# A two-direction gated recurrence: one direction of two heads per tile instead of both directions of one head

## The chip, the cores and the metric

The program runs on one core of one Trainium2 chip. The metric is device time in microseconds (us) for one execution of the whole program. TensorE is called PE, its weight loads PEld, VectorE DVE, ScalarE ACT, GpSimd POOL; SP issues most DMAs.

## The reference, cut to what matters

The program is a trunk of two layers over 512 latent and 256 context tokens of width 1024. Each layer applies a norm, one input projection, four token mixers (A to D), an output projection and a mixture of experts. The change lies in mixer A, a gated linear recurrence with 4 heads of 64 channels, run forwards and backwards over the tokens:

```python
def step(S, inp):                      # one chunk of 64 tokens, one direction
    qc, kc, fc, vc = inp
    b = jnp.cumsum(fc, axis=2)         # log decays
    o_inter = einsum('bhtk,bhkv->bhtv', qc * exp(b), S)
    decay = exp(where(causal, b[t] - b[s], -inf))
    attn = einsum('bhtk,bhsk,bhtsk->bhts', qc, kc, decay)
    o_intra = einsum('bhts,bhsv->bhtv', attn, vc)
    S_new = exp(b_last) * S + einsum('bhsk,bhsv->bhkv', kc * exp(b_last - b), vc)
...
o_f, _ = hgrn_chunk_scan(qh, k_f, lf_f, ih, s_cf)
o_b, _ = hgrn_chunk_scan(rev(qh), rev(k_b), rev(lf_b), rev(ih), s_cb)
out = hgrn_readout(o_f + rev(o_b), g, norm_g)
```

The query is the same in both directions; forget gates and keys differ. Layer 0 computes outputs for all 768 tokens (NQ = 768), layer 1 for the 512 latent ones (NQ = 512); states run over 768 in both.

## The kernel before, in words

Channels lie on partitions, tokens along the free axis. `Proj.cols` (line 1281) makes 128 columns of the input projection at a time; an `ev` function moves them out of PSUM. For the recurrence these are two tiles of values, two of queries, four of gates and two of output gates. The queries of each head are written twice (lines 1530 and 1531): rows 0 to 63 of a tile `QQ[h]` for the forward direction, rows 64 to 127 for the backward one. Gate tile h holds the forward channels of head h in rows 0 to 63 and its backward channels in rows 64 to 127; from it come the decays `F[h]` and the keys `K[h]`.

`hgrn` then works in five steps.

1. Level 0, per head: `scores` multiplies keys and queries of each 128 tokens (line 234, NP = 6 or 4 matmuls of 128 rows, into a double PSUM bank from a ring of two), DVE keeps the diagonal (line 239), and the queries are multiplied by F (line 246).
2. Six levels with half-blocks of 1, 2, 4, ... 32 tokens; at each, four heads. ACT builds `kx`: the keys of the half-block that a direction reads from, and zeros in the other half (lines 256 and 257, two instructions each on 64 partitions). `scores` multiplies; DVE copies the valid pairs into the score tile A with a predicated copy (line 241). Then queries and keys are decayed in place: the forward rows on DVE, the backward rows on POOL, a query multiply (line 265) and a key multiply (line 266) each. DVE merges the block decays T (line 268).
3. Per pair of heads and head: the keys are transposed (line 278), copied by ACT (line 279), multiplied by the values with 64 rows at a time (line 284), and DVE scans the states over 12 chunks, forwards in rows 0 to 63 and backwards in rows 64 to 127 (line 291, 22 instructions per head).
4. Values times scores (line 300) and states times queries (line 303) give the outputs in PSUM.
5. Square, head sum (line 309), reciprocal root and gate (lines 194 to 200, 312, 313).

One fp32 matmul of the program appears in the trace as two records, each with its weight load. A scheduler puts the instructions of each engine in a fixed order: work that is later in the program fills an engine where the earlier work is expected to wait. In the levels this filling is the modulation (line 1175, `more(STEPH)`) and the Hyena projection (line 1281). Both follow `hgrn` in the program.

Of the kernel before, what the change touches and what calls it, by code (L numbers as in the profile page):

```python
# [25 lines left out]
class Region:  # L26
    """First-fit allocation of columns of one SBUF tile, in program order."""
# [26 lines left out]
class Arena:  # L54
    """The regions that are open at a point of the program; later ones are filled first."""
# [27 lines left out]
class Scope:  # L83
    """Named rings of arena buffers that live together."""
# [30 lines left out]
class Env:  # L115
    """Memory and small helpers shared by the stages."""
# [34 lines left out]
    def px(self):  # L151
        """One bank, of the two kinds in turn."""
# [6 lines left out]
    def pf(self):  # L159
        """One bank, of the single and double kinds in turn."""  # L160
# [6 lines left out]
    def load(self, tag, ap, bufs=1):  # L167
        """Arena copy of a DRAM array [128 or fewer, ...]."""
# [11 lines left out]
def split(n):  # L180
    """Column ranges of at most one PSUM bank."""
# [7 lines left out]
def rsqrt_wide(E, src, n, scale, tag, tags=None, width=NTOK):  # L189
    """1/sqrt(scale*src + EPS) for src [128, n] (PSUM): Ln/Exp estimate and one Newton step."""  # L190
# [13 lines left out]
# ---------------------------------------------------------------- HGRN  # L204
# [4 lines left out]
def hgrn_masks():  # L209
    """Valid (s, t) pairs of a 128-token chunk pair: the diagonal, then each level, both directions."""  # L210
# [7 lines left out]

def hgrn(E, need_ctx, QQ, F, K, V, SG, gn, oT):
# [7 lines left out]
    A, QR, T = {}, {}, {}  # L227
    fw, bw = slice(0, 64), slice(64, 128)

    def scores(h, lev, kx, q):  # L230
        ps = E.p2()
        for p in range(NP):
            c = slice(p * 128, p * 128 + 128)
            nc.tensor.matmul(ps[:, c], kx[:, c], q[:, c], start=True, stop=True)  # L234
        m = masks[:, lev, :].unsqueeze(1).to_broadcast([P, NP, 128])
        pv = ps[:, :NQ].rearrange("p (a t) -> p a t", t=128)
        if lev == 0:
            A[h] = E.t("hA", NTOK, bufs=4)
# [1695 lines left out]
```

## Time and profile before

| | us |
|---|---|
| median of three runs | 2461.23 |
| lowest and highest | 2455.57, 2463.83 |
| profiled execution, first to last instruction (its span) | 2456.8 |
| recurrence levels, layer 0 (258 to 322) | 64 |
| recurrence levels, layer 1 (1498.5 to 1553.5) | 55 |

The page of the profile gives no time of that execution beside its span; the span lies inside the runs shown, 4.4 us under their median. In the profile "busy" is the time in which an engine worked on at least one instruction, so instructions that overlap count once; a mean duration counts each instruction in full. Matmul ends are modelled.

### The profile page before, as it was taken

What the parts mean: (1) busy time and instruction counts of PE and PEld (TensorE: products, weight loads), DVE (VectorE), ACT (ScalarE), POOL (GpSimd) and SP (SyncE); (2) the same over time, 40 slices, a digit from 0 to 9 for tenths busy, and PEclk for the clock granted to TensorE, in tenths of its full rate; (3) what the DMA queues carried; (4) which work ended last, traced back from release to release, by engine and by line L of the source; (5) the groups of instructions that cost most, each with busy time, mean ns of one, the idle gap of its engine ahead of it and who ended that gap; (6) DMA issues with size and microseconds to landing.
All of it is one profiled execution on the core that took longest, in us unless ns stands there. A gap on an engine that the chain in (4) does not pass through costs nothing.

```text
span 2456.8 us, 32343 instructions
## 1 busy us (share of the span) xinstructions
PE 2056.0 (84%) x11460; PEld 1197.4 (49%) x11460; DVE 1053.5 (43%) x2495; ACT 606.9 (25%) x1200; POOL 587.5 (24%) x477
## 2 busy tenths in 40 slices
PE   5889888998999588887777498899999588877776
PEld 1557667865679333322222286676668433222221
DVE  6760985546865622221111437754684611111111
ACT  3434632243541100000000235324352110000000
POOL 1552722312003211211111236331101212111111
PEclk9999999999999699999999799999999699999998
DMA  6434424301231899999999524431233799999996
GB/s 244 156 121 163 172 81 148 112 26 52 84 130 70 290 385 376 405 402 404 400 402 400 216 86 155 134 125 35 73 116 116 283 391 409 411 407 410 410 406 263
DMA packets 139315, 581.56 MB, mean 237 GB/s; under 512 B 23984, under 2 KB 47873, under 8 KB 88630
## 3 DMA queue, kind: packets, MB, share of 16 engines
q1 hardware_dynamic: 124054, 555.89, 58.4%
q0 software_dynamic: 15008, 22.36, 3.8%
q8 instruction: 151, 2.47, 0.4%
q14 instruction: 102, 0.84, 0.1%
HBM read 554.17 MB, written 36.80 MB: 241 GB/s over the span
## 4 chain that ended last, share of the span: by engine, by line
DMA 20%; PE 19%; another core or an unknown queue 18%; DVE 8%; issue 2%; ACT 1%; POOL 1%; SPq 0%; ACTq 0%; POOLq 0%; DVEq 0%
DMA acc<-arena 8%; DMA out_dram<-arena 7%; PE pw L1281 6%; DMA arena<-h2d,arena 4%; PE pb L993 3%; PE pw L1773 2%; PE pb L1020 1%; PE pb L607 1%; PE pb L509 1%; PE pb L527 1%; DVE arena L265 1%; DMA arena<-in_w_out 1%; DVE arena L266 1%; PE pb L1748 0%
## 5 line engine op out<-in xcount | busy, mean ns | idle before, releaser
L993 PE MATMUL pb<-side,arena 128*64 128x512 f32 x1224 | 287.1, 603 | 43.0 <-DMA side<-in_w_moe 40.9
L997 DVE COPY arena<-pb 128x512 f32<-128x512 f32 x67 | 46.4, 692 | 496.0 <-PE pb L993 496.0
L993 PE MATMUL pb<-arena 128*64 128x512 f32 x920 | 217.1, 605 | 40.5 <-DMA arena<-in_w_moe 36.9
L1009 ACT ACTIVATE arena<-pb 128x256 f32<-128x256 f32 x67 | 25.7, 383 | 900.1 <-PE pb L1006 900.1
L1257 POOL TENSOR_TENSOR wl<-side,wh 128x1024 fp32r<-128x1024 f32 x52 | 126.4, 2430 | 380.2 <-ACT wh L1256 225.9
L993 PEld LDWEIGHTS pb<-side,arena 128*64 128x64 f32 x1224 | 81.2, 137 | 243.4 <-issue 126.6
L1281 PE MATMUL pw<-hh,wh 128*128 128x512 f32 (+1 forms) x720 | 170.7, 371 | 2.6 <-ACT arena L1180 1.2
L1281 PE MATMUL pw<-hh,wl 128*128 128x512 f32 (+1 forms) x720 | 163.1, 359 | 0.0
L1024 DVE SCALAR_TENSOR_TENSOR arena<-pb,arena 128x512 f32<-128x512 f32 x67 | 50.3, 751 | 262.9 <-PE pb L1020 253.0
L1281 PE MATMUL pw<-hl,wh 128*128 128x512 f32 (+1 forms) x720 | 160.5, 357 | 0.0
L993 PEld LDWEIGHTS pb<-arena 128*64 128x64 f32 x920 | 62.1, 138 | 189.0 <-issue 100.2
L1020 PE MATMUL pb<-side,arena 128*64 128x512 f32 x576 | 134.3, 606 | 23.6 <-DVE arena L1010 21.5
L1033 POOL DMA_INDIRECT acc<-arena x35 | 55.2, 1577 | 384.6 <-DVE arena L1028 344.5
L1281 PEld LDWEIGHTS pw<-hh,wh 128*128 128x128 f32 x720 | 120.4, 194 | 36.1 <-issue 12.5
L1020 PE MATMUL pb<-arena 128*64 128x512 f32 x496 | 117.2, 613 | 21.7 <-DVE arena L1010 20.6
L1281 PEld LDWEIGHTS pw<-hl,wh 128*128 128x128 f32 x720 | 118.2, 190 | 25.0 <-issue 8.9
L1281 PEld LDWEIGHTS pw<-hh,wl 128*128 128x128 f32 x720 | 117.6, 189 | 24.6 <-issue 9.7
L1033 POOL DMA_INDIRECT out_dram<-arena x32 | 50.9, 1590 | 311.1 <-DVE arena L1024 299.1
L971 POOL DMA_INDIRECT arena<-h2d,arena x67 | 69.8, 1042 | 187.0 <-issue 65.6
L1777 POOL TENSOR_TENSOR arena<-arena 128x256 f32<-128x256 f32 x40 | 30.4, 759 | 294.3 <-DVE arena L1776 185.5
L234 PE MATMUL pa<-arena 128*128 128x128 f32 x560 | 75.6, 283 | 18.5 <-ACT arena L257 6.0
L1006 PE MATMUL pb<-ident,arena 128*128 128x128 f32 x268 | 42.2, 280 | 56.3 <-DVE arena L997 55.4
(368 smaller groups left out, 3594.3 us busy)
## 6 DMA issues: line engine op xcount, KB each, us to landing
side<-in_w_moe SPq DMA_DIRECT2D x215, 1024.0 KB
arena<-in_w_moe SPq DMA_DIRECT2D x169, 1024.0 KB
arena<-in_w_ada SPq DMA_DIRECT2D x53, 512.0 KB
side<-in_w_in SPq DMA_DIRECT2D x52, 512.0 KB
side<-in_w_ada SPq DMA_DIRECT2D x43, 512.0 KB
arena<-in_w_out SPq DMA_DIRECT2D x16, 512.0 KB
arena<-in_x SPq DMA_DIRECT2D x12, 512.0 KB
spd<-arena SPq DMA_DIRECT2D x23, 256.0 KB
```

The lines of the kernel that those rows point to most:

```text
L234: nc.tensor.matmul(ps[:, c], kx[:, c], q[:, c], start=True, stop=True)
L971: E.gathered = nc.gpsimd.indirect_dma_start(out=xg, out_offset=None, in_=h2d, in_offset=bass.IndirectOffsetOnAxis(ap=gi, axis=0), **(dict( ...
L993: nc.tensor.matmul(pg[64 * s:64 * s + 64], xT[:, j // 4, j % 4, :], W[j // 2][:, (j % 2) * 1024 + s * 512:(j % 2) * 1024 + s * 512 + 512], ...
L997: nc.vector.tensor_copy(gu, pg)
L1006: nc.tensor.transpose(pt[:, c * 128:(c + 1) * 128], gu[:, c * 128:(c + 1) * 128], E.c["ident"])
L1020: nc.tensor.matmul(pd[64 * s:64 * s + 64], hT[:, c, :], W[4 + c // 2][:, (c % 2) * 1024 + s * 512:(c % 2) * 1024 + s * 512 + 512], start=( ...
L1024: nc.vector.scalar_tensor_tensor(y, pd, w[0], g2[0], op0=ALU.mult, op1=ALU.mult)
L1033: E.nc.gpsimd.indirect_dma_start(out=acc, out_offset=bass.IndirectOffsetOnAxis(ap=si, axis=0), in_=y, in_offset=None, compute_op=ALU.add, ...
L1257: (nc.vector if k % 2 else nc.gpsimd).tensor_sub(lo, src, hi.bitcast(F32))
L1281: nc.tensor.matmul(ps[:, :n], w[:, j, :], h[:, j, a:a + n], start=(i == 0), stop=(i == 23))
L1773: nc.tensor.matmul(ps[:, :256], o_[:, k, tt], w[:, k, :], start=(i == 0), stop=(i == 23))
L1777: nc.gpsimd.tensor_add(x1[t][:, cc], x1[t][:, cc], tmp)
```

## The change

A tile now holds one direction of two heads: `K[2*pair]` is the forward keys of both heads of a pair (head 0 in rows 0 to 63, head 1 in rows 64 to 127), `K[2*pair+1]` their backward keys; F likewise. The columns of the weights and the lower-bound logits are put in that order on the host. The queries come out of the projection as they are, one ACT copy per chunk, two tiles instead of four; a second copy per pair arises when they are multiplied by F.

At level 0 each head's scores are the sum of two products of 64 rows, forward and backward keys. At each level a merged key tile `mk` and a merged query tile `mq` are built by four ACT copies on 128 partitions per pair: the forward keys of the first half-blocks beside the backward keys of the second, and the reverse for queries. Nothing is zeroed. The scores are matmuls of 64 rows per head that alternate between the two heads, into both double banks of the ring. Query decays all run on DVE, key decays all on POOL, with 128 partitions each. After the levels, the transposed keys, the last block decays and the queries are rearranged back to both directions of one head by ACT copies (`kts`, `Th`, `QB`), since the scan is as before.

```diff
-    def scores(h, lev, kx, q):
-        ps = E.p2()
+    def scores(pair, lev, terms):
+        ps = [E.p2() for _ in range(2)]
         for p in range(NP):
             c = slice(p * 128, p * 128 + 128)
-            nc.tensor.matmul(ps[:, c], kx[:, c], q[:, c], start=True, stop=True)
+            for s, rows in enumerate(half):
+                for i, (k, q) in enumerate(terms):
+                    nc.tensor.matmul(ps[s][:, c], k[rows, c], q[rows, c], start=(i == 0), stop=(i == len(terms) - 1))
...
-    for h in range(4):
-        scores(h, 0, K[h], QQ[h])
-        QR[h] = QQ[h]
-        nc.vector.tensor_mul(QR[h][:, :NQ], QQ[h][:, :NQ], F[h][:, :NQ])
-        T[h] = F[h]
+    QR = {}
+    for pair in range(2):
+        f, b = 2 * pair, 2 * pair + 1
+        scores(pair, 0, [(K[f], Q[pair]), (K[b], Q[pair])])
+        QR[f], QR[b] = E.t("hQR", NTOK, bufs=2), Q[pair]
+        nc.vector.tensor_mul(QR[f][:, :NQ], Q[pair][:, :NQ], F[f][:, :NQ])
+        nc.vector.tensor_mul(QR[b][:, :NQ], Q[pair][:, :NQ], F[b][:, :NQ])
+        T[f], T[b] = F[f], F[b]
...
-        for h in range(4):
-            kx = E.t("hKX", NTOK, bufs=2)
...
-            for rows, src in ((fw, 0), (bw, 1)):
-                nc.scalar.copy(xv[rows, :nq, src, :], kv[rows, :nq, src, :])
-                nc.scalar.activation(xv[rows, :nq, 1 - src, :], kv[rows, :nq, src, :], AF.Copy, scale=0.0)
-            scores(h, li + 1, kx, QR[h])
...
-            for rows, mine, other in ((fw, 1, 0), (bw, 0, 1)):
-                eng = nc.vector if rows is fw else nc.gpsimd
...
-                eng.tensor_mul(qv[rows, :nq, mine, :], qv[rows, :nq, mine, :], tq)
-                eng.tensor_mul(kv[rows, :, other, :], kv[rows, :, other, :], tk)
-            T[h] = F[h][:, :nb] if hb < 32 else E.t("hT", nb, bufs=4)
-            nc.vector.tensor_mul(T[h], tv[:, :, 0], tv[:, :, 1])
+        for pair in range(2):
+            f, b = 2 * pair, 2 * pair + 1
+            mq, mk = E.t("hKT", NTOK, bufs=2), E.t("hKX", NTOK, bufs=2)
+            for dst, first, second in ((mk, K[f], K[b]), (mq, QR[b], QR[f])):
+                for i, src in enumerate((first, second)):
+                    nc.scalar.copy(blocks(dst)[:, :nq, i, :], blocks(src)[:, :nq, i, :])
+            scores(pair, li + 1, [(mk, mq)])
+            for z, mine in ((f, 1), (b, 0)):
...
+                nc.vector.tensor_mul(qv[:, :nq, mine, :], qv[:, :nq, mine, :], tq)
+                nc.gpsimd.tensor_mul(kv[:, :, 1 - mine, :], kv[:, :, 1 - mine, :], tk)
+                T[z] = F[z][:, :nb] if hb < 32 else E.t("hT", nb, bufs=4)
+                nc.vector.tensor_mul(T[z], tv[:, :, 0], tv[:, :, 1])
...
     for pair in range(2):
...
+        for r, rows in enumerate(half):
+            z = 2 * pair + r
+            ps = E.p2()
+            for t in range(6):
+                nc.tensor.transpose(ps[:, t * 128:(t + 1) * 128], K[z][:, t * 128:(t + 1) * 128], ident)
+            pv = ps[:, :NTOK].rearrange("p (t s c) -> p t s c", t=6, s=2)
+            for s in range(2):
+                nc.scalar.copy(kts[s][:, :, r], pv[:, :, s])
+                nc.scalar.copy(Th[s][rows], T[z][half[s]])
...
+            QB[s] = K[h]
+            for r, rows in enumerate(half):
+                nc.scalar.copy(QB[s][rows, :NQ], QR[2 * pair + r][half[s], :NQ])
...
-                def ev(ps, a, n):
-                    for s_ in range(2):
-                        q = QQ[2 * pair + s_]
-                        nc.vector.tensor_copy(q[0:64, a:a + n], ps[64 * s_:64 * s_ + 64])
-                        nc.scalar.copy(q[64:128, a:a + n], ps[64 * s_:64 * s_ + 64])
-                pr.cols(COL["q"] + pair, both, ev)
+                pr.cols(COL["q"] + pair, both, lambda ps, a, n: nc.scalar.copy(QQ[pair][:, a:a + n], ps))
```

## Rows read from the trace of the kernel before

**Rows 1.** Busy time by stretch: PE, PEld, DVE, ACT, POOL, clock, DMA share, GB/s.

```profile
258.00:322.00 64.00, 53.79 (x451) 39.23 (x451) 64.00 (x91) 45.87 (x98) 49.53 (x54) 1.00 0.47 163
322.00:346.00 24.00, 18.81 (x191) 15.16 (x190) 18.49 (x57) 4.59 (x7) 3.17 (x2) 0.86 0.23 79
...
1498.50:1553.50 55.00, 45.39 (x374) 28.66 (x366) 55.00 (x99) 37.40 (x100) 44.62 (x54) 1.00 0.60 199
1553.50:1580.00 26.50, 25.95 (x205) 18.59 (x204) 18.03 (x52) 6.74 (x10) 4.55 (x2) 1.00 0.39 124
```

**Rows 2.** Groups by line and shape, 258 to 322 (busy us, mean ns, idle before).

```profile
L234 PE MATMUL pa<-arena 128*128 128x128 f32 x277 | 36.7, 282 | 9.9 <-ACT arena L257 3.2 <-DVE arena L241 2.3 <-DVE arena L268 1.8
...
L266 POOL TENSOR_TENSOR arena<-arena 64x384 f32<-64x384 f32 x22 | 23.3, 1057 | 11.9 <-ACT arena L257 9.1 <-DVE arena L266 2.2 <-DVE arena L265 0.6
L241 DVE COPY_PREDICATED arena<-hmask,pa 128x768 f32<-128x768 uint32 x23 | 23.2, 1007 | 0.0
L256 ACT COPY arena<-arena 64x384 f32<-64x384 f32 x44 | 22.9, 522 | 20.0 <-PE pa L234 11.4 <-DVE arena L266 7.2 <-PE pw L1175 0.8
L265 DVE TENSOR_TENSOR arena<-arena 64x384 f32<-64x384 f32 x23 | 19.5, 846 | 0.0
L266 DVE TENSOR_TENSOR arena<-arena 64x384 f32<-64x384 f32 x22 | 17.6, 798 | 0.0
...
L268 DVE TENSOR_TENSOR arena<-arena 128x24 f32<-128x24 f32 x4 | 2.8, 709 | 0.0
...
L268 DVE TENSOR_TENSOR arena<-arena 128x96 f32<-128x96 f32 x4 | 0.9, 236 | 0.0
```

**Rows 3.** The same view, 1498.5 to 1553.5 (layer 1).

```profile
L234 PE MATMUL pa<-arena 128*128 128x128 f32 x184 | 26.2, 285 | 8.2 <-ACT arena L257 2.8 <-DVE arena L241 2.2 <-DVE arena L268 1.5
...
L266 DVE TENSOR_TENSOR arena<-arena 64x384 f32<-64x384 f32 x24 | 18.1, 755 | 0.0
...
L265 DVE TENSOR_TENSOR arena<-arena 64x256 f32<-64x256 f32 x24 | 17.9, 747 | 0.0
L241 DVE COPY_PREDICATED arena<-hmask,pa 128x512 f32<-128x512 uint32 x24 | 17.2, 717 | 0.0
```

**Rows 4.** Single lines, both layers: duration ns min/median/max, first and last start.

```profile
L265 DVE TENSOR_TENSOR arena<-arena x48: 401/587/1535, 259.7 to 1552.6; 64x384 f32<-64x384 f32 x24, 64x256 f32<-64x256 f32 x24
L266 DVE TENSOR_TENSOR arena<-arena x48: 540/544/1561, 260.2 to 1552.9; 64x384 f32<-64x384 f32 x48
L268 DVE TENSOR_TENSOR arena<-arena x48: 153/335/814, 261.6 to 1553.4; 128x384 f32<-128x384 f32 x8, 128x192 f32<-128x192 f32 x8, 128x96 f32<-128x96 f32 x8, 128x48 f32<-128x48 f32 x8
L239 DVE TENSOR_TENSOR arena<-pa,hmask x8: 677/818/958, 251.2 to 1497.9; 128x768 f32<-128x768 f32 x4, 128x512 f32<-128x512 f32 x4
L246 DVE TENSOR_TENSOR arena<-arena x8: 941/1061/1504, 252.1 to 1498.5; 128x768 f32<-128x768 f32 x4, 128x512 f32<-128x512 f32 x4
```

**Rows 5.** Timeline, start, length and merged count; idle before in brackets.

```profile
272.63 1.58 PE L234 MATMUL pa<-arena 128*128 128x128 f32 x12 [1.06 <-POOL arena L289]
...
326.13 0.80 ACT L279 COPY arena<-pa 128x768 f32<-128x768 f32 x1 [2.45 <-PE pa L278]
326.98 1.42 PEld L284 LDWEIGHTS pa<-arena 64*128 64x128 f32 x24 [0.40 <-ACT arena L279]
326.98 1.55 PE L284 MATMUL pa<-arena 64*128 64x64 f32 x24
...
328.46 1.01 PEld L1281 LDWEIGHTS pw<-hh,wh 128*128 128x128 f32 x8
```

**Rows 6.** Groups by line and shape on PE, the whole span.

```profile
L993 PE MATMUL pb<-side,arena 128*64 128x512 f32 x1224 | 287.1, 603 | 43.0 <-DMA side<-in_w_moe 40.9 <-ACT arena L983 1.4 <-SPq L1110 0.3
...
L309 PE MATMUL pa<-arena,ones 128*128 128x512 f32 x8 | 4.3, 617 | 0.0
```

**Rows 7.** Busy time by stretch as in rows 1, two stretches after the levels.

```profile
332.00:334.00 2.00, 0.00 (x0) 0.00 (x0) 1.81 (x7) 0.86 (x2) 2.00 (x1) 1.00 0.00 0
...
338.00:340.00 2.00, 2.00 (x17) 0.78 (x18) 1.83 (x6) 0.05 (x1) 0.00 (x0) 0.50 0.00 0
```

More of the change, by code (lines that the diff above doesn't have):

```diff
@@ L216, in hgrn_masks, with hgrn @@
     return np.stack(out, 1).astype(np.float32)
-def hgrn(E, need_ctx, QQ, F, K, V, SG, gn, oT):
+def hgrn(E, need_ctx, Q, F, K, V, SG, gn, oT):
     nc = E.nc
@@ L270, in hgrn @@
     ident = E.c["ident"]
     for pair in range(2):
-        S, VA = {}, {}
+        kts = [E.t("hKT", NTOK, bufs=2).rearrange("p (t d c) -> p t d c", t=6, d=2) for _ in range(2)]
+        Th = [E.t("hTh", NTOK // 64, bufs=4) for _ in range(2)]
+        for r, rows in enumerate(half):
[4 more added lines that the diff above has]
+            pv = ps[:, :NTOK].rearrange("p (t s c) -> p t s c", t=6, s=2)
+            for s in range(2):
+                nc.scalar.copy(kts[s][:, :, r], pv[:, :, s])
+                nc.scalar.copy(Th[s][rows], T[z][half[s]])
@@ L273, in hgrn @@
+        S, QB = {}, {}
         for s in range(2):
             h = 2 * pair + s
-            kt = E.t("hKT", NTOK, bufs=2)
-            ps = E.p2()
-            for t in range(6):
-                nc.tensor.transpose(ps[:, t * 128:(t + 1) * 128], K[h][:, t * 128:(t + 1) * 128], ident)
-            nc.scalar.copy(kt, ps[:, :NTOK])
+            kt = kts[s].rearrange("p t d c -> p (t d c)")
             pk = E.p2()
@@ L285, in hgrn @@
                                      V[rr, t, h * 64:h * 64 + 64], start=True, stop=True)
+            QB[s] = K[h]
+            for r, rows in enumerate(half):
+                nc.scalar.copy(QB[s][rows, :NQ], QR[2 * pair + r][half[s], :NQ])
             st = F[h]
             S[s] = st
-            for rows, seq in ((fw, [8, 9, 10, 11, 0, 1, 2, 3, 4, 5, 6, 7]), (bw, [11, 10, 9, 8, 7, 6, 5, 4, 3, 2, 1, 0])):
+            for rows, seq in ((half[0], [8, 9, 10, 11, 0, 1, 2, 3, 4, 5, 6, 7]),
+                              (half[1], [11, 10, 9, 8, 7, 6, 5, 4, 3, 2, 1, 0])):
                 nc.gpsimd.memset(st[rows, seq[0] * 64:seq[0] * 64 + 64], 0.0)
@@ L291, in hgrn @@
                     nc.vector.scalar_tensor_tensor(st[rows, b * 64:b * 64 + 64], st[rows, a * 64:a * 64 + 64],
-                                                   T[h][rows, a:a + 1],
+                                                   Th[s][rows, a:a + 1],
                                                    pk[rows, (a % 2) * 512 + (a // 2) * 64:(a % 2) * 512 + (a // 2) * 64 + 64],
@@ L1524, in trunk @@
             pr.rows(COL["i"], V, False, "hKT", 2)
-            QQ = [E.t("hQQ", NTOK, bufs=4) for _ in range(4)]
+            QQ = [E.t("hQQ", NTOK, bufs=2) for _ in range(2)]
             for pair in range(2):
-                def ev(ps, a, n):
-                    for s_ in range(2):
-                        q = QQ[2 * pair + s_]
-                        nc.vector.tensor_copy(q[0:64, a:a + n], ps[64 * s_:64 * s_ + 64])
-                        nc.scalar.copy(q[64:128, a:a + n], ps[64 * s_:64 * s_ + 64])
-                pr.cols(COL["q"] + pair, both, ev)
+                pr.cols(COL["q"] + pair, both, lambda ps, a, n: nc.scalar.copy(QQ[pair][:, a:a + n], ps))
             F = [E.t("hF", NTOK, bufs=4) for _ in range(4)]
@@ L1861, in layout @@
     lb = i["hgrn_lb_logits"].reshape(2, 2, 4, 64)
-    d["lbl"] = lb.transpose(1, 3, 2, 0).reshape(128, 4, 2)
+    d["lbl"] = lb.reshape(2, 2, 2, 2, 64).transpose(3, 4, 2, 1, 0).reshape(128, 4, 2)
     wg, wu, wd = i["moe_w_gate"], i["moe_w_up"], i["moe_w_down"]
@@ L1870, in layout @@
     cols = []
-    for h in range(4):
-        cols += [hs(256, h), hs(512, h)]
+    for pair in range(2):
+        for base in (256, 512):
+            cols += [hs(base, 2 * pair), hs(base, 2 * pair + 1)]
     cols = [np.arange(768, 1024)] + cols
```

30 lines of the change are left out of this document (15 added, 15 removed).

## The prediction

> **What bounds the kernel now.** I read the page first, then busy time by stretch, then the groups by line and shape in the two stretches where the changed levels run, then single lines for their shortest and longest times, and the timeline where a group's mean could not decide. In both stretches DVE is busy all the time, 64.0 of 64.0 us in layer 0 and 55.0 of 55.0 in layer 1 [rows 1]. PE is busy for 53.8 and 45.4 us, but only 36.7 and 26.2 of that are the scores [rows 2, 3]; the rest, about 17 and 19 us, is filling work from later in the program. So two things set what a change is worth here: DVE sets the length of the levels, and the sum of PE's work and PE's idle time sets when everything after them comes, because PE is the engine that stays busiest after the levels (18.8 of 24 and 26.0 of 26.5 us [rows 1]). PE idles 10.2 and 9.6 us within the levels.
>
> **DVE in the levels.** Per head and level DVE runs one predicated copy, one query multiply, one key multiply and one merge of T. In layer 0 the groups are 23.2 + 19.5 + 17.6 us, and six T groups, of which the dearest took 2.8 and the cheapest 0.9, add 10.4 [rows 2]: 70.7 us of durations in 64.0 us of busy time, so 0.905 of a sum is real time, as neighbours overlap. In layer 1 the groups shown are 17.2 + 17.9 + 18.1, T took 8.3 and other work 2.7: 64.2 in 55.0, or 0.857 [rows 1, 3].
>
> The multiplies have two kinds of duration: the key multiply is 0.540 us at the least and 0.544 in the median, but 0.798 on average in layer 0 and up to 1.56 [rows 2, 4]. The long ones lie beside POOL multiplies of 1.06 us on the same kind of data [rows 2]; I read them as waits for POOL.
>
> *After, layer 0.* The 24 predicated copies stay: 24 x 1.007 = 24.2. Four query multiplies per level (two pairs, two directions) on 128 partitions are 24 in all, of the same 384 elements per partition: 24 x 0.54 = 13.0. The 24 merges of T stay: 24 x 0.335 = 8.0 by the median. All 22 to 24 key multiplies leave DVE. The excess over unblocked multiplies is 23 x 0.31 + 22 x 0.26 = 12.8 us now, beside two POOL multiplies per head and level; POOL's count halves (key multiplies only, 384 elements as now, about 1.06 each), and DVE's too, so I keep 5 us of it (bounds 0 and 12.8). Sum 50.2 x 0.905 = 45 us, with bounds 41 and 52.
>
> *After, layer 1.* 24 x 0.717 + 24 x 0.401 (the shortest of the 256-element query multiplies [rows 4]) + 8.0 + 5 = 39.8, x 0.857 = 34 us, with bounds 30 and 41.
>
> **PE in the levels, the uncertain price.** Per pair and level there are still 12 (layer 1: 8) matmuls of 128 columns, so 24 (16) records, now of 64 rows, alternately in the upper and the lower half of the rows. Twelve full-height records take 1.58 us, 0.132 each; 24 records of 64 rows that alternate the same way, but move 64 columns, take 1.55, 0.065 each [rows 5]. That can mean two halves at work at once, or only half as many columns; 0.065 and 0.132 are the bounds for a 128-column record. The nearest row where a half array can be priced is the expert product: 64 of the 128 array columns, 512 columns moved, 287.1 / 1224 = 0.235 us, against 4.3 / 8 = 0.54 for the full array [rows 6]. Halves of the array evidently overlap there, so I take 0.065: 24 x 0.065 = 1.56 us per pair and level in layer 0, 1.04 in layer 1. The Trainium skill, "TensorEngine Tiling (Array Packing)", section Key Properties, states that different tiles can load and multiply in parallel; no row here shows that for halves of the rows.
>
> PE's own work in the levels falls to 12 x 1.56 = 18.7 us (from 36.7) and 12 x 1.04 = 12.5 (from 26.2).
>
> Against the alternating shapes speaks a row and a rule. The first full-width load after the 64-row group starts at 328.46, and the last 64-row load ends at 326.98 + 1.42 = 328.40, so a change of shape cost 0.06 us there [rows 5]. The same section of the skill says that changing the tiling mode drains TensorE. By that rule two changes at each of the 24 pair-levels of both layers would add 48 x 0.06 = 2.9 us; the row bears out a cost this small, and as today's scores already alternate with other shapes, my sum takes none.
>
> **The new wait.** A pair's scores now take both double banks of the ring. PE can't begin the other pair before DVE has copied the first one out; before, it could work a head ahead. Behind that wait on PE stand the filling matmuls; the score copies on DVE wait for it. The loop per pair and level in layer 0 is scores 1.56 + two copies 2 x 1.007 + two hand-overs. For one of those I take 0.2 (the load at 326.98 follows the end of ACT's copy at 326.93 by 0.05 [rows 5]; a matmul's end adds its pipeline). That is 4.0 us, x 12 = 48. In layer 1, 1.04 + 1.43 + 0.4 = 2.9, x 12 = 35. While PE multiplies, DVE has two query multiplies and two merges, 1.8 us, to do. So the loop (48, 35) and DVE's load (45, 34) nearly coincide. They won't interleave perfectly: I take 50 and 38 us in place of 64 and 55, which is -14 and -17.
>
> ACT and POOL don't bind: ACT's four instructions per pair and level are 4 x 0.522 = 2.1 us [rows 2] in loops of 4.2 (now 46 of 64 us are busy, after about 30); POOL's two are 2.1. Both stay under the loop. The query multiplies no longer wait for the scores, since the matmuls read copies.
>
> **Level 0.** Now PE works ahead and DVE sets the pace: 1.6 + 4 x (0.96 + 1.06) = 9.7 us in layer 0 [rows 4, 5]. After, a pair needs 48 records, 3.1 us, and the second pair waits for the two masks of the first: 3.1 + 0.2 + (1.9 + 0.2 + 3.1 + 0.2) + 4.0 = 12.7, so +3. In layer 1: 2.1 + 0.2 + (1.4 + 0.2 + 2.1 + 0.2) + 3.4 = 9.6 for 7.8, so +2.
>
> **After the levels.** The scan of a pair waits for both transposes and four copies instead of one transpose and one copy of 0.80 [rows 5]. That is one more transpose group, about 0.85 by the 12 records above, and 4 short copies plus 4 tiny ones for 0.8: about +1.5 us for the first pair of each layer. For the second pair DVE's scan of the first covers it. The four `QB` copies, some 0.8 each, lie beside the scan of 44 DVE instructions; ACT is busy 4.6 of 24 us there [rows 1]. Without that cover they would cost 3.2 per pair. Sum +3 for both layers.
>
> **Query evacuation.** Two DVE and two ACT instructions per chunk become one ACT instruction. PE's 48 and more projection matmuls per column tile hide either; without that cover two ACT copies of about 0.6 per chunk would be at stake. I count nothing.
>
> **Sum.** -14 - 17 + 3 + 2 + 3 = -23 us. As a check by PE: its work falls by 18.0 + 13.7 = 31.7. With the same filling (17 and 19) it is idle 50 - 18.7 - 17 = 14 and 38 - 12.5 - 19 = 6.5 us in the levels, against 10.2 and 9.6, nearly the same total, so -31 before the +8. What follows is shifted as a whole: the expert weights need the memory that the attentions free. Against its own span of 2456.8 this gives 2434; the median of the runs stands 4.4 higher, so 2461.2 - 23 = **2438 us**.
>
> **Rivals.**
> 1. *PE gives everything back* (chance 0.08). The order fills the shorter waits so well that PE's idle time also halves, about 10 us: -31.7 - 10 + 3 = -39, 2422. For it: much work stands ready behind. Against it: a fixed order left 20 us idle even now.
> 2. *The filling does not follow* (0.12). If the order is made as though a score record still took 0.132, the scores fill 12 x 3.17 = 38 us of a loop of 48 (25 of 35 in layer 1), and about 10 us of filling fit in each. PE then idles 50 - 18.7 - 10 = 21 and 15.5 us, and the rest of the filling comes later: (-18 + 11) + (-13.7 + 6) + 8 = -7, 2454. For it: the order is fixed before the run. Half of this chance is on the faster side of the bound.
> 3. *The row halves do not overlap* (0.12), so the change makes no score cheaper. Loop 24 x 0.132 + 2.0 + 0.4 = 5.6 x 12 = 67 us and 2.1 + 1.4 + 0.4 = 3.9 x 12 = 47, so +3 - 8; level 0 has 48 (32) records per pair at 0.132, +8 and +5; with the +3, +11: 2472. It decides from about 0.11 us per record, where the gain is gone. For it: the 64-row group's time is exactly what 64 columns alone would give. Against it: halves of the array columns overlap [rows 6].
> 4. *The clock* (0.06). After the idle stretch 332 to 334 the granted clock was 0.50 in 338 to 340, that is 1.2 GHz [rows 7]. With less work PE waits more in the levels; at 1.2 GHz throughout, its 36 and 32 us become 72 and 63, plus 8 is +24, 2485. It decides when over half of both stretches is at that level. Against it: the clock was 1.00 with PE 84% busy [rows 1], and the new waits are about 2.4 us, with filling in them.
>
> **How the numbers follow.** The forecast has 0.62, its own range 2424 to 2450 (levels 44 and 34 at best, 58 and 44 at worst). A measurement of this kernel can tell about 0.3%, 7.4 us. Faster: 0.62 + 0.08 + 0.06 = 0.76. Same: 0.06 from rival 2, 0.02 from rival 3, 0.01 from rival 4: 0.09. Slower: 0.10 + 0.05 = 0.15. The range 2416 to 2464 holds the forecast and rivals 1 and 2 and leaves out rivals 3 and 4, 0.18 in all.
>
> **What the profile will show.** Right: no DVE key multiply in the levels, DVE below 100% there, stretches near 50 and 38 us, a 64-row 128-column record at about 0.065 us, POOL about half as busy, long multiplies rarer. Wrong: records at 0.13, PE idle over 20 us in a stretch, a clock of 0.5 in the levels, or a longer gap on PE before the outputs at line 300, where the order already left some 5 us idle [rows 1].

## The result, and the profile after

After the change the kernel takes 2417.49 us in the median of four runs (2414.06 to 2423.79), against 2462.53 of four runs of the kernel before: ratio 0.983, 95% interval 0.9806 to 0.9854. The gain is 45 us by the medians and 42 by the ratio, where the sum said 23. The time lies in the stated range, near its lower end, 6.5 us below the forecast's own range, and next to the price of the first rival (2422).

Lines have moved: the scores are L237 (L234 before), masks L244, predicated copies L246, ACT's copies L265, query multiplies L272, key multiplies L273, merges of T L275, scan L310, outputs L319 and L322, and the transforms after layer 0's recurrence L528 and L546 (L509 and L527).

Engine totals of the page of the changed kernel:

```profile
span 2418.0 us, 32200 instructions
...
PE 2039.0 (84%) x11540; PEld 1186.2 (49%) x11540; DVE 999.4 (41%) x2435; ACT 573.2 (24%) x1138; POOL 537.2 (22%) x429
```

Before, PE was busy for 2056.0 of 2456.8 us. So PE works 17.0 us less, and the span without PE work falls from 400.8 to 379.0, another 21.8.

Where the 38.8 us of span lie, by first starts of the same work in both traces (the attention's first inputs are the matmul of L729, after L748):

| | before | after | difference | the sum said |
|---|---|---|---|---|
| layer 0: first mask at | 251.2 | 246.4 | -4.8 | 0 |
| first mask to first scan | 74.6 | 60.1 | -14.5 | -14 + 3 |
| first scan to the attention's first inputs | 165.8 | 157.5 | -8.3 | +1.5 |
| layer 1: first mask at | 1492.7 | 1467.1 | lead 25.6 | |
| first mask to first scan | 61.8 | 47.9 | -13.9 | -17 + 2 |
| first scan to the attention's first inputs | 119.5 | 121.9 | +2.4 | +1.5 |

From layer 0's attention to layer 1's mask it is 2.0 us longer, and behind layer 1's attention 1.6 shorter. The two stretches of levels, level 0 included, came out near the forecast, -28.4 for -26. The rest of the miss lies outside them: ahead of layer 0's mask, and above all behind layer 0's levels.

Busy time by stretch of the changed kernel, the two stretches of levels and, between them, the one behind layer 0's levels (columns as in [rows 1]):

```profile
256.80:306.50 49.70, 47.64 (x446) 35.89 (x446) 41.31 (x67) 23.55 (x61) 19.27 (x22) 0.90 0.54 185
306.50:334.30 27.80, 24.08 (x198) 19.31 (x197) 18.56 (x56) 10.63 (x15) 2.34 (x1) 0.88 0.17 58
1475.60:1515.00 39.40, 33.56 (x360) 22.57 (x354) 33.46 (x68) 20.17 (x63) 19.45 (x23) 0.94 0.70 238
```

They last 49.7 and 39.4 us (50 and 38 were forecast), with DVE busy for 41 and 33 (45 and 34). DVE is no longer busy all the time, and POOL is busy for 19 us instead of 49.5 and 44.6 [rows 1].

Groups by line and shape in the first of these stretches, as in [rows 2]:

```profile
L237 PE MATMUL pa<-arena 64*128 64x128 f32 x264 | 29.0, 310 | 2.1 <-DVE arena L246 2.1
...
L246 DVE COPY_PREDICATED arena<-hmask,pa 128x768 f32<-128x768 uint32 x24 | 23.1, 1014 | 4.5 <-PE pa L237 4.5
L273 POOL TENSOR_TENSOR arena<-arena 128x384 f32<-128x384 f32 x20 | 19.0, 969 | 19.4 <-ACT arena L265 15.9 <-DVE arena L246 3.4
L265 ACT COPY arena<-arena 128x384 f32<-128x384 f32 x38 | 16.9, 515 | 15.5 <-PE pa L237 15.4
L272 DVE TENSOR_TENSOR arena<-arena 128x384 f32<-128x384 f32 x20 | 15.7, 823 | 0.6 <-ACT arena L265 0.6
```

The scores take 29.0 us instead of 36.7, not 18.7: a record of 64 rows costs 0.110 on average. With the other 18.6 us of PE's work that leaves PE 2.1 us idle, where the prediction had 14. The timeline shows the loop, here one pair every 3.4 to 3.6 us and 3.8 on average over the layer's twelve (4.0 was forecast), and 24 records in 2.4:

```profile
276.05 2.42 PE L237 MATMUL pa<-arena 64*128 64x128 f32 x24
...
278.30 1.94 DVE L246 COPY_PREDICATED arena<-hmask,pa 128x768 f32<-128x768 uint32 x2
...
279.49 2.41 PE L237 MATMUL pa<-arena 64*128 64x128 f32 x24
...
283.04 2.48 PE L237 MATMUL pa<-arena 64*128 64x128 f32 x24
```

The two copies of a pair ran from 278.30 to 279.35 and from 279.24 to 280.24. The next pair's scores began at 279.49, behind the first copy and beside the second.

### The profile page after: what moved, and what is told of

It reads as the page before. It is cut to its first block, busy times and chain, and to the rows that moved or that the text cites. A ratio compares the mean times of both kernels' runs of the same rounds, so it can differ in the third digit from the quotient of the medians.

```text
span 2418.0 us, 32200 instructions
## 1 busy us (share of the span) xinstructions
PE 2039.0 (84%) x11540; PEld 1186.2 (49%) x11540; DVE 999.4 (41%) x2435; ACT 573.2 (24%) x1138; POOL 537.2 (22%) x429
## 5 line engine op out<-in xcount | busy, mean ns | idle before, releaser
L1012 PE MATMUL pb<-side,arena 128*64 128x512 f32 x1224 | 288.9, 604 | 45.9 <-DMA side<-in_w_moe 42.2
L1016 DVE COPY arena<-pb 128x512 f32<-128x512 f32 x67 | 46.3, 691 | 501.5 <-PE pb L1012 501.5
L1012 PEld LDWEIGHTS pb<-side,arena 128*64 128x64 f32 x1224 | 81.4, 137 | 246.5 <-issue 126.4
L1039 PE MATMUL pb<-side,arena 128*64 128x512 f32 x576 | 137.8, 617 | 24.9 <-DVE arena L1029 20.4
L1039 PEld LDWEIGHTS pb<-side,arena 128*64 128x64 f32 x576 | 39.0, 140 | 101.5 <-issue 60.8
```

The lines of the kernel that those rows point to most:

```text
L1012: nc.tensor.matmul(pg[64 * s:64 * s + 64], xT[:, j // 4, j % 4, :], W[j // 2][:, (j % 2) * 1024 + s * 512:(j % 2) * 1024 + s * 512 + 512], ...
L1016: nc.vector.tensor_copy(gu, pg)
L1039: nc.tensor.matmul(pd[64 * s:64 * s + 64], hT[:, c, :], W[4 + c // 2][:, (c % 2) * 1024 + s * 512:(c % 2) * 1024 + s * 512 + 512], start=( ...
```

## The experiments

Ratios are to the kernel before, timed in the same series, with 95% intervals. "Stretch" is first mask to first scan, layer 0 and layer 1: 74.6 and 61.8 before, 60.1 and 47.9 after.

**Is the earlier mask worth anything?** Two runs move the copies of the queries out of PSUM between DVE and ACT. In the kernel before:

```diff
-                        nc.vector.tensor_copy(q[0:64, a:a + n], ps[64 * s_:64 * s_ + 64])
+                        nc.scalar.copy(q[0:64, a:a + n], ps[64 * s_:64 * s_ + 64])
```

> The kernel before, with one edit: all four query copies of a chunk run on ACT, none on DVE. Theory (the saving starts before the recurrence: the DVE copies stood behind spectrum work that waits for a DMA, PE stood still 3.8 us in layer 0 and came back at the lower clock): the gap at 186.7 to 190.5 goes, the first mask comes 3 to 5 us earlier, and the time is 3 to 5 us lower, 2457 to 2460 beside 2462. Rival (any evacuation in four pieces is too long, or ACT stands behind the same spectrum work): the gap stays or grows, time the same or up to 3 us higher.

Measured: 2460.36, ratio 1.0002 (0.9988 to 1.0016). The first mask comes 2.5 us earlier, the attention's first inputs 5.0, and the end not at all. In the kernel after:

```diff
-lambda ps, a, n: nc.scalar.copy(QQ[pair][:, a:a + n], ps))
+lambda ps, a, n: nc.vector.tensor_copy(QQ[pair][:, a:a + n], ps))
```

> The changed kernel, with the one query copy of each chunk on DVE instead of ACT. Theory (the DVE queue is what held the queries up): PE stands still again before the gates in layer 0, 3 to 5 us are given back, 2420 to 2423 beside 2417.5. Rival (the gap came from the number of pieces, four per chunk, on two engines): no gap, 2416 to 2419.

Measured: 2416.91, ratio 0.9819 (0.9801 to 0.9837), as with the copy on ACT. The first mask is back at 251.19, and still nothing is lost at the end. What this edit wins early is given back later; counting nothing for it was right, though a milestone moves.

**Does it matter that POOL has left the queries' path?**

```diff
-                nc.vector.tensor_mul(qv[:, :nq, mine, :], qv[:, :nq, mine, :], tq)
-                nc.gpsimd.tensor_mul(kv[:, :, 1 - mine, :], kv[:, :, 1 - mine, :], tk)
+                (nc.vector if mine else nc.gpsimd).tensor_mul(qv[:, :nq, mine, :], qv[:, :nq, mine, :], tq)
+                (nc.vector if mine else nc.gpsimd).tensor_mul(kv[:, :, 1 - mine, :], kv[:, :, 1 - mine, :], tk)
```

> The changed kernel, but query and key multiplies split by direction as before: forward ones on DVE, backward ones on POOL. DVE and POOL have the same number of instructions as in the changed kernel (24 each per layer). Theory (part of the saving is that POOL no longer stands in the path of the queries, so that PE waits less): the stretch from first mask to first scan grows by 2 to 6 us per layer, 2422 to 2430. Rival (only the count of multiplies on DVE matters): within 3 us of 2417.5.

Measured: 2415.51, ratio 0.9809 (0.9788 to 0.983), stretches 60.3 and 46.0. The rival holds: it makes no difference to the time which 24 of the 48 multiplies POOL has.

**Does DVE's load set the levels after the change?** The forward keys go back to DVE, then all keys:

```diff
-                nc.gpsimd.tensor_mul(kv[:, :, 1 - mine, :], kv[:, :, 1 - mine, :], tk)
+                (nc.vector if mine else nc.gpsimd).tensor_mul(kv[:, :, 1 - mine, :], kv[:, :, 1 - mine, :], tk)
```

> The changed kernel, but the forward key multiplies (12 per layer) go back from POOL to DVE. Theory (DVE's load sets the length of the levels): 12 x 0.54 to 0.8 us more on DVE per layer, less what overlaps: first mask to first scan 4 to 8 us longer per layer, 2425 to 2433. Rival (the loop of scores, two copies out of PSUM and hand-overs sets it, and DVE has idle time for them, 41 of 50 us busy now): within 3 us of 2417.5.

Measured: 2409.08 (2406.52 to 2412.46), ratio 0.9782 (0.9761 to 0.9803), the best of all kernels here; stretches 57.2 and 44.3. With 12 more multiplies per layer on DVE the levels become shorter, which neither the theory nor the rival had. Groups by line and shape of that run, 256.5 to 304.8:

```profile
L272 DVE TENSOR_TENSOR arena<-arena 128x384 f32<-128x384 f32 x21 | 11.7, 573 | 0.6 <-ACT arena L265 0.6
L273 POOL TENSOR_TENSOR arena<-arena 128x384 f32<-128x384 f32 x10 | 9.7, 970 | 28.0 <-ACT arena L265 28.0
...
L273 DVE TENSOR_TENSOR arena<-arena 128x384 f32<-128x384 f32 x10 | 5.6, 559 | 0.0
```

With half of POOL's multiplies gone, the query multiply of DVE takes 0.573 on average instead of 0.823.

```diff
-                nc.gpsimd.tensor_mul(kv[:, :, 1 - mine, :], kv[:, :, 1 - mine, :], tk)
+                nc.vector.tensor_mul(kv[:, :, 1 - mine, :], kv[:, :, 1 - mine, :], tk)
```

> The changed kernel, with all key multiplies on DVE and none on POOL. With half of them on DVE the time fell to 2409, and the query multiplies went from 0.78 to 0.57 us. Theory A (POOL beside DVE is what costs; without POOL no multiply waits): DVE's load is 24.2 + 13 + 13 + 7 = 57 x 0.9 = 52 us in layer 0 and about 44 in layer 1, against stretches now of 49.7 and 39.4, so 1 to 4 us per layer longer than with half, 2410 to 2417. Theory B (POOL's key multiplies stand in the chain to the next copies, and DVE is quicker there): shorter again, 2400 to 2407. Theory of the prediction (DVE's load sets the levels): 2425 to 2440.

Measured: 2415.13, ratio 0.9816 (0.9799 to 0.9834), stretches 58.0 and 46.3, as theory A had it. Busy time by stretch of its levels in layer 0:

```profile
254.90:303.80 48.90, 44.99 (x467) 33.98 (x456) 45.32 (x88) 24.80 (x62) 0.58 (x4) 1.00 0.55 192
```

DVE runs 48 multiplies, 24 predicated copies and 24 merges here, as many as before the change, in 45.3 us of a stretch of 48.9. Before, the same counts kept it busy for all of 64.0 [rows 1]. The work of these instructions did not fill that time; what ran beside them stretched them.

**How much of the gain does DVE's relief give by itself?** The kernel before, without DVE's key multiplies:

```diff
                 eng.tensor_mul(qv[rows, :nq, mine, :], qv[rows, :nq, mine, :], tq)
-                eng.tensor_mul(kv[rows, :, other, :], kv[rows, :, other, :], tk)
+                if rows is bw:
+                    eng.tensor_mul(kv[rows, :, other, :], kv[rows, :, other, :], tk)
```

> The kernel before, leaving out the key multiplies of the forward rows, the 48 that ran on DVE (the forward keys stay undecayed); everything else stays. It prices the one thing that the change takes off DVE. Theory of the prediction (in the kernel before DVE's load sets the levels, so most of the saving is these multiplies): first mask to first scan 74.6 to about 60 in layer 0 and 61.8 to about 47 in layer 1, time 2425 to 2435. Rival A (the waits of scores for POOL and ACT set the levels): 2 to 6 us shorter per layer, 2448 to 2458. Rival B (the levels shorten and PE's idle time behind them, 15.1 us in layer 0, shrinks too): 2415 to 2425.

Measured: 2445.76, ratio 0.9942 (0.9924 to 0.9959), stretches 64.6 and 53.8. A third of the gain; it lies between what the theories had expected.

**And with POOL's query multiplies left out as well?**

```diff
-                eng.tensor_mul(qv[rows, :nq, mine, :], qv[rows, :nq, mine, :], tq)
-                eng.tensor_mul(kv[rows, :, other, :], kv[rows, :, other, :], tk)
+                if rows is fw:
+                    eng.tensor_mul(qv[rows, :nq, mine, :], qv[rows, :nq, mine, :], tq)
+                else:
+                    eng.tensor_mul(kv[rows, :, other, :], kv[rows, :, other, :], tk)
```

> The kernel before, leaving out DVE's key multiplies (forward half) and POOL's query multiplies (backward half), so that DVE and POOL each run 24 multiplies per layer in the levels, as after the change. The score matmuls stay at 128 rows, ACT's four copies per head and level and all buffers stay as before. The output is not the reference's. Theory A (what the change wins in the levels is the halved number of multiplies on both engines): from the first mask to the first scan 58 to 61 us in layer 0 and 46 to 49 in layer 1, as after the change, against 64.6 and 53.8 where DVE's key multiplies alone were left out; time 2414 to 2430. Rival B (the merged operands, ACT's fewer copies or PE's halved records carry what DVE's relief did not): stretches of 63 us or more and 52 or more, time 2436 to 2450.

Measured: 2434.78, ratio 0.9897 (0.9875 to 0.9919), stretches 61.4 and 48.1. The stretches are nearly those of the change, as theory A had it; the time is not, it lies just outside rival B's range. So halving the multiplies on both engines shortens the levels by nearly all that the change shortens them, and some 17 us of the gain come from elsewhere. The trace shows where half of that lies: from the first scan to the attention's inputs this kernel still takes 166.0 us in layer 0 (157.5 after the change), with PE idle for 13.6 (15.2 before, 7.5 after). The rest is not placed.

One row here matters for the cause. POOL runs 24 multiplies per layer as after the change, but DVE's query multiply is not stretched. Groups by line and shape, 256.9 to 310.8:

```profile
L266 DVE TENSOR_TENSOR arena<-arena 64x384 f32<-64x384 f32 x24 | 13.0, 542 | 0.0
```

So the number of POOL's multiplies does not set DVE's time by itself; it counts whether they meet.

**Do ACT's fewer copies matter?**

```diff
-                nc.scalar.activation(xv[rows, :nq, 1 - src, :], kv[rows, :nq, src, :], AF.Copy, scale=0.0)
```

> The kernel before, leaving out the 48 ACT instructions per layer that write zeros into the key copies, so that ACT runs 48 copies in the levels, as after the change. The output is not the reference's. Theory (ACT lies under DVE's load, as the prediction had it): DVE still sets the levels, 72 us or more and 60 or more from first mask to first scan, time 2453 to 2464. Rival (POOL's key multiply, for which 9 us of POOL's idle time end at ACT's zeroing copy, carries ACT's delay on to the next level): stretches of 68 and 56 or less, time 2438 to 2450.

Measured: 2456.11, ratio 0.9975 (0.9962 to 0.9989), stretches 75.8 and 62.7. The levels do not become shorter, so ACT lay under the others there; the 6 us gained lie behind layer 1's levels (112.4 us to the attention's inputs for 119.5), and why is open. The run shows more than that. Busy time by stretch, layer 0, and two of its groups:

```profile
259.50:327.80 68.30, 57.25 (x483) 42.12 (x483) 68.30 (x99) 26.88 (x54) 49.13 (x54) 1.00 0.45 150
```

```profile
L265 DVE TENSOR_TENSOR arena<-arena 64x384 f32<-64x384 f32 x24 | 29.0, 1207 | 0.0
...
L264 DVE TENSOR_TENSOR arena<-arena 64x384 f32<-64x384 f32 x24 | 15.0, 627 | 0.0
```

POOL's key multiply waits less for ACT here (3.1 us, for 9.1 in [rows 2]), and DVE is again busy all the time; only, DVE's key multiply (L265 in this kernel) now takes 1.207 on average instead of 0.798 [rows 2]. Its busy time is no measure of its work.

**What does POOL's load cost in the kernel after?** Each key multiply in two halves of 64 partitions, so that POOL has 48 multiplies per layer again:

```diff
-                nc.gpsimd.tensor_mul(kv[:, :, 1 - mine, :], kv[:, :, 1 - mine, :], tk)
+                for rows in half:
+                    nc.gpsimd.tensor_mul(kv[rows, :, 1 - mine, :], kv[rows, :, 1 - mine, :], tk[rows])
```

> The kernel after, with each POOL key multiply of 128 partitions issued as two of 64 partitions, so that POOL again runs 48 multiplies per layer, each of 384 elements per partition, as before the change. Nothing else moves. Theory A (POOL's load, in DVE's way and on the keys' path, is a large part of what the change wins): the stretches from mask to scan grow by 3 us or more each, from 60.1 and 47.9, and DVE's query multiplies take 0.9 us or more on average instead of 0.82; time 2426 to 2440. Rival B (POOL lies under the loop of scores and copies, with 19 of 50 us busy): 60 and 48 as they are, time 2414 to 2421.

Measured: 2443.9, ratio 0.9931 (0.9911 to 0.9952), stretches 73.8 and 63.0: those of the kernel before, with everything else of the change in place. 26 of the 45 us are gone, more than theory A had. Groups by line and shape (the query multiply is L272, the key multiply L274, the merge L276), and busy time by stretch, layer 0:

```profile
L274 POOL TENSOR_TENSOR arena<-arena 64x384 f32<-64x384 f32 x40 | 40.1, 1002 | 12.0 <-ACT arena L265 9.7
...
L272 DVE TENSOR_TENSOR arena<-arena 128x384 f32<-128x384 f32 x20 | 19.1, 996 | 0.3 <-ACT arena L265 0.3
...
L276 DVE TENSOR_TENSOR arena<-arena 128x24 f32<-128x24 f32 x4 | 0.6, 181 | 3.3 <-POOL arena L274 3.3
```

```profile
259.90:319.70 59.80, 54.23 (x444) 40.98 (x446) 46.26 (x66) 22.68 (x58) 40.38 (x42) 0.76 0.44 154
...
280.00:284.00 4.00, 2.00 (x20) 1.36 (x20) 3.20 (x6) 1.75 (x4) 3.70 (x5) 1.00 0.50 171
284.00:288.00 4.00, 4.00 (x36) 2.51 (x34) 4.00 (x8) 2.02 (x5) 2.34 (x3) 0.61 0.04 11
288.00:292.00 4.00, 4.00 (x32) 3.55 (x34) 2.15 (x4) 0.34 (x1) 2.51 (x3) 0.50 0.72 252
```

DVE's query multiply grows to 0.996, and merges wait for POOL. Part of the loss is TensorE's clock: after 280 to 284, where PE was busy for half of the time, the granted clock falls to 0.50, that is 1.2 GHz, and over the stretch it is 0.76 (0.90 with POOL's 24 multiplies). The run prices POOL's load together with that clock. The step from the kernel without DVE's key multiplies to the one without POOL's query multiplies too, where the clock stayed at 1.00 in the levels, prices the query multiplies without it: 0.9942 to 0.9897, 11 us.

**Do the two halves of the rows overlap?** First with all 128 rows in each matmul, which sums both heads in each score:

```diff
-nc.tensor.matmul(ps[s][:, c], k[rows, c], q[rows, c], start=(i == 0), stop=(i == len(terms) - 1))
+nc.tensor.matmul(ps[s][:, c], k[:, c], q[:, c], start=(i == 0), stop=(i == len(terms) - 1))
```

> The changed kernel, with the score matmuls over all 128 rows instead of 64 (each head's scores become the sum over both heads), so that no two of them can run at once; counts and copies stay. Theory (the halves do overlap, 0.10 us per record, and PE's time in the loop matters): records at 0.13, loop 24 x 0.03 us longer per pair and level, PE work 13 and 7 us more: 2428 to 2438. Rival (records of 64 rows are as dear as full ones in the loop, the overlap is worth nothing): within 3 us of 2417.5.

Measured: 2421.49, ratio 0.9846 (0.9822 to 0.9871), stretches 61.8 and 48.8: 4 us lost where the theory had 10 to 20. Then in the kernel after with turns of two blocks per head:

```diff
-        for p in range(NP):
-            c = slice(p * 128, p * 128 + 128)
+        for p0 in range(0, NP, 2):
             for s, rows in enumerate(half):
...
+                for p in (p0, p0 + 1):
+                    c = slice(p * 128, p * 128 + 128)
```

> The changed kernel, with the score matmuls in another order: two blocks of 128 tokens of one head, then two of the other, instead of one and one. At level 0, where four records in a row lie in the same half, a record took 0.064 to 0.078 us, in the levels with two in a row 0.09 to 0.10. Theory (the length of the run in one half sets how well the halves overlap): 0.065 to 0.08 in the levels, the stretch 3 to 6 us shorter per layer, 2408 to 2414. Rival (something else in the levels, such as the copies beside, slows the records): 0.09 to 0.10 still, 2415 to 2420.

Measured: 2427.92, ratio 0.9872 (0.9856 to 0.9889), stretches 57.5 and 48.4. Both expectations miss. The 10 us are lost behind layer 1's levels (134.5 us to the attention's inputs for 121.9), where PE now waits for transfers of weights and once 5.55 us for DVE; the records in the levels are as before (24 in 1.93 to 2.50 us). Last, all blocks of one head ahead of the other's, with the forward keys on DVE as in the best run:

```diff
-        for p in range(NP):
-            c = slice(p * 128, p * 128 + 128)
-            for s, rows in enumerate(half):
+        for s, rows in enumerate(half):
+            for p in range(NP):
+                c = slice(p * 128, p * 128 + 128)
```

> The kernel after, with the forward key multiplies on DVE, as in the run that came out at 2409, and with the six score matmuls of the first head issued ahead of the six of the second, instead of one by one in turn. Theory A (the loop of scores and predicated copies sets the levels now): the first copy can begin when half of the 64-row records are done, 1.1 us earlier in layer 0 and 0.8 in layer 1 at each of 12 pairs and levels; if half of that shows, stretches of 51 and 40 instead of 57.2 and 44.3, time 2395 to 2403. Rival B (records of the same row half do not overlap with each other, so that two turns of 0.13 take the place of 0.10 and eat the earlier start, or PE's work sets the end): time 2405 to 2413.

Measured: 2433.12, ratio 0.988 (0.9861 to 0.99), stretches 54.4 and 49.8: 24 us slower than with the heads in turn, so theory A fell, and by more than rival B had it. The first of the stretches becomes shorter, the second longer. The scores of the whole span, by line, in the kernels before, after, with full rows, with forward keys on DVE, and with these by head:

```profile
L234 PE MATMUL pa<-arena 128*128 128x128 f32 x560 | 75.6, 283 | 18.5 <-ACT arena L257 6.0 <-DVE arena L241 4.5 <-DVE arena L268 3.3
```

```profile
L237 PE MATMUL pa<-arena 64*128 64x128 f32 x640 | 63.0, 299 | 8.7 <-DVE arena L246 3.9 <-ACT arena L265 2.0 <-DVE arena L244 1.4
```

```profile
L237 PE MATMUL pa<-arena 128*128 128x128 f32 x640 | 78.9, 279 | 3.7 <-DVE arena L246 1.7 <-ACT arena L1199 0.9 <-ACT arena L290 0.7
```

```profile
L237 PE MATMUL pa<-arena 64*128 64x128 f32 x640 | 59.3, 285 | 3.8 <-DVE arena L246 1.9 <-ACT arena L265 0.8 <-DVE arena L244 0.8
```

```profile
L237 PE MATMUL pa<-arena 64*128 64x128 f32 x640 | 74.2, 288 | 1.3 <-DVE arena L246 0.8 <-DVE arena L244 0.3
```

Busy time through count is 0.135 us per record before, 0.098 after, 0.123 with full rows, 0.093 in the best kernel and 0.116 by head. The mean of one, from start to modelled end, is nearly the same in all five; what differs is how far neighbours overlap. By head they hardly do: in layer 0's levels, at a clock of 1.00 in both kernels, 264 records took 26.1 us in turn and 273 took 30.8 by head. Layer 1's clock of 0.88 has a part in the rest.

The 14.9 us more of scores are not the loss by themselves: full rows add 15.9 (78.9 for 63.0) and lose 4 us. By head, PE is idle for only 0.3 us from layer 0's mask to its scan, and PE's records other than scores fall there from 225 to 164, and in layer 1 from 202 to 162. They come behind the levels instead: from the first scan to the attention's inputs layer 0 takes 169.0 us for 156.7, with 61 records more. That the displaced filling is the loss fits these counts; no run tests it apart.

In turn, the overlap is for the most part whole or absent. Three groups of the kernel after, at a clock of 1.00, by timeline: level 0's first pair, a pair of layer 0's levels, a pair of layer 1's:

```profile
243.68 2.95 PE L237 MATMUL pa<-arena 64*128 64x128 f32 x46
...
279.49 2.41 PE L237 MATMUL pa<-arena 64*128 64x128 f32 x24
...
1480.68 1.17 PE L237 MATMUL pa<-arena 64*128 64x128 f32 x16
```

The first and the last take 0.064 and 0.073 per record: their records start two by two, some 0.01 apart, one such couple every 0.11. In the middle group the first seven records start one by one, 0.11 apart, as full rows do, until the second copy ends at 280.24; couples come from 280.85 on. So the mean of 0.10 is a mixture of the two. The trace does not name a record's half; that the first records are those of the head whose bank came free first is read from these times.

## Why the prediction was off, step by step

The range held, but the stretches of levels came out near their forecast by errors that cancel, and that is luck.

**The levels: right in size, wrong in the reason.** The forecast of -14 and -17 for them, with +3 and +2 for level 0, came out as -14.5 and -13.9 in all (level 0, first mask to first predicated copy, +2.9 and +1.5). But "DVE sets the length of the levels" does not stand. It rested on DVE being busy for 64.0 of 64.0 us [rows 1], and a good part of that was waiting inside instructions: the multiplies' excess over 0.54, 12.8 us, was in the sum, and was called a wait for POOL there. The step that failed is the next one, "ACT and POOL don't bind". What decides is the pair: POOL's 48 multiplies per layer, and DVE's beside them. With POOL's load put back the stretches are those of before (73.8 and 63.0); with POOL's load gone and DVE's count as before they are 58.0 and 46.3. A row that was at hand pointed there. Before, the weight loads of layer 0's scores stood mostly for POOL, as the view of the single line L234 shows (idle before it, times, by who ended it; PE and its weight loads together, of POOL's 20.5 us all but 1.5 before loads; PE's own row in [rows 2] names ACT and DVE first, so this is a hint, and the runs are the evidence):

```profile
  POOL arena L265: 11.3, 9
  POOL arena L266: 9.2, 12
  ACT arena L257: 3.7, 4
  DVE arena L241: 2.3, 6
```

After, no score waits for POOL.

The Trainium skill, "SBUF — State Buffer", section "Who interferes with whom", states that a DVE instruction with two SBUF inputs contends with a GpSimd instruction that reads SBUF. The traces agree. The query multiplies, which have two such inputs, took 0.543 in layer 0's levels with no multiply on POOL and in the new layout 0.573 with 12 per layer, 0.823 with 24 and 0.996 with 48, while the predicated copy out of PSUM stayed between 1.00 and 1.03. It is the meeting that costs, not the count: with 24 on POOL in the old layout they took 0.542. Sorted one by one, DVE's products of 384 elements in layer 0's levels took at most 0.56 us after the change where no POOL product ran beside them (13 of 26) and 0.975 on average where one did; in the kernel before 13 of 52 ran free, at most 0.55, and the others took 0.887.

**The record of 64 rows: mis-sized.** 0.065 was taken; it measured 0.090 to 0.105 where 24 records ran at full clock in layer 0's levels, 0.098 over the span. As an estimate for two halves at work at once 0.065 was right: level 0's first pair has it. In the levels part of a pair's records run alone, by the reading above because one head's bank comes free before the other's, and the sum left that out. So PE's own work on the scores fell by 12.6 us (75.6 to 63.0, level 0 included), not by 31.7.

**The new wait: wrong in its terms.** "PE can't begin the other pair before DVE has copied the first one out" put scores and both copies end to end. With the measured 2.4 for the scores that loop would be 4.8 us, and by rival 3 the gain would be gone at about 0.11 per record. It took 3.4 to 3.6 in the rows shown, because the next scores begin behind the first copy and run beside the second. The dearer record and the shorter loop cancel, so that PE's idle time in the levels fell to 2.1 us instead of rising to 14. Rival 3, no overlap at all, was wrong in its price for the same reason: with full rows, where a record takes 0.123, the kernel loses 4 us, with intervals that overlap, and not 34. (Its +8 and +5 for level 0 are a little low too; the prediction's own formula gives some +9 and +6.)

**"Nearly the same total" of PE's idle time: wrong.** Outside PE's work the span lost 21.8 us. From first mask to first scan PE idled 10.2 and 9.9 us before and 2.8 and 7.4 after; behind layer 0's levels it was 15.2 and is 7.5. Another 6.5 lie between layer 0's attention and layer 1's mask, where nothing was gained, since that stretch became 2.0 us longer. The run with half the multiplies in the old layout has 0.5 and 1.2 in the stretches, so relief of DVE and POOL takes PE's waits out of the levels; those behind layer 0's levels go by another cause (next step). Rival 1, that the order's filling follows so well that PE's waits shrink too, came nearest, with other terms: less of PE's work saved, more of its idle time.

**After the levels: the sign was wrong in layer 0.** Forecast +1.5, measured -8.3 there and +2.4 in layer 1. The extra transposes were counted, and no wait was thought to go. Waits went: before, PE stood 4.23 us for the first pair's scan, where the prediction had counted 1.5 more, 1.23 for the second pair's and 2.86 for the transform's table; after, it is 2.38 for the first, and the other two have no gap. From the timelines of before and after:

```profile
335.82 0.69 PE L300 MATMUL pa<-arena 128*64 128x128 f32 x2 [4.23 <-DVE arena L291]
...
371.42 0.43 PE L300 MATMUL pa<-arena 128*64 128x128 f32 x2 [1.23 <-DVE arena L291]
...
404.93 0.70 PE L509 MATMUL pb<-arena 128*128 128x256 f32 x2 [2.86 <-DMA arena<-in_hy_fwd]
```

```profile
315.97 0.40 PE L319 MATMUL pa<-arena 128*64 128x128 f32 x2 [2.38 <-DVE arena L310]
...
386.77 1.13 PE L528 MATMUL pb<-arena 128*128 128x256 f32 x4
```

The table's load was issued 8.3 us ahead of its first use before (396.66) and 17.0 after (369.82). That belongs to the new layout and not to speed: with halved multiplies in the old one PE stood 2.81 us at the same place, and with slow levels in the new one (POOL's load put back) not at all, and PE's idle time behind layer 0's levels was 7.1. All five kernels of the old layout show this wait in layer 0 (1.9 to 2.9 us), and none of the nine of the new one. In layer 1 it did not go: 1.39 before, 2.78 after. In both traces SP issues the load close behind the store of the last outputs (395.81 and 368.36), which comes 8.2 us sooner after the first scan in the new layout; what in the layout brings that about was not tried and stays open, and so does the shorter wait of the first pair.

**Query copies: nothing, as forecast.** The mask's 4.8 us are theirs (251.19 again with the copy on DVE), but no run shows them at the end.

**The clock: in part.** Rival 4 named it with a price for half of both stretches. After the change it was 0.90 and 0.94, which made two groups of 24 score records in layer 0 take 3.9 us each instead of 2.4, and only with POOL's load put back 0.76 and 0.77.

Put together, by ratio times 2461: DVE's keys 14, POOL's queries 11, the new layout 13 (from 0.9897 to 0.9846, where matmuls still have full rows), the half rows 4. The first two are shown by leaving out the work. The third is the difference of two kernels that share the levels' lengths; no run takes the layout's parts one by one. The fourth lies within what the intervals leave open.

## What to carry to other kernels

A busy share of 100% on DVE beside a busy POOL is no proof that DVE's work fills the time: compare each group's mean with its shortest instance, and read who released the matmuls, before an engine is called the bound. When one of two engines that block each other is relieved, price the pair, and try the work on one of them alone: here half the key multiplies back on DVE gave 2409 us, better than the kernel before and the one after. A change of layout also moves the waits behind the loop that it is about; list the gaps that stand there now and ask for each whether it will still be there.

## What the runs showed of the hardware

Matmuls of 64 rows and 128 columns took 0.064 us per record where the upper and the lower half of the rows ran side by side throughout (46 records in 2.95 us), 0.123 with all 128 rows, and 0.116 over the span where four or six of one half follow each other. Records of one half in series started 0.11 us apart, as those of full rows did, so half the rows alone save nothing. Over the span it was 0.098 in the kernel after and 0.093 in the best one, where only a part of the records ran side by side. A DVE multiply that took 0.54 us alone took up to 1.207 in the mean beside POOL multiplies, all of it shown as busy time.
